# Latent up projection: rotary columns of q's weights stored twice, rotation in two operations, k's plain columns scaled on POOL, rotary squares inside k's sum

## The chip, the cores and the metric

The kernel runs on one core of a Trainium2 chip. The core has five engines that work side by side, each with its own queue of instructions that it takes in order: TensorE (PE, matrix products; its weight loads are shown as PEld), VectorE (DVE), ScalarE (ACT), GpSimd (POOL) and SyncE (SP), which here issues the transfers between the chip's main memory and the on-chip memory SBUF. Matrix products land in a second on-chip memory, PSUM, which POOL does not read in this kernel.

The metric is the time of one execution in microseconds (us), median of several runs. Before the change it is 1326.62 us (3 runs, 1322.44 to 1329.13).

## The reference

One layer of a streaming encoder, batch 1, sequence 1024, width 1024: an adaptive normalisation, a mixer with two groups of heads (latent attention "mla" and banded chunk attention), and a gated MLP with a causal convolution. The change lies in how q and k of the latent attention are made:

```python
MLA_HEADS = 8; MLA_NOPE = 64; MLA_ROPE = 32; MLA_QK = 96

q = jnp.dot(rmsnorm(q_lat, g_q_latent), w_q_up).reshape(B, S, MLA_HEADS, MLA_QK)
kv = jnp.dot(rmsnorm(kv_lat, g_kv_latent), w_kv_up).reshape(B, S, MLA_HEADS, MLA_NOPE + MLA_V)
k_nope, v = kv[..., :MLA_NOPE], kv[..., MLA_NOPE:]
k = jnp.concatenate([k_nope, jnp.broadcast_to(k_rope[:, :, None, :], (B, S, MLA_HEADS, MLA_ROPE))], axis=-1)
q = rmsnorm(q, g_mla_q)
k = rmsnorm(k, g_mla_k)
q = jnp.concatenate([q[..., :MLA_NOPE], rope(q[..., MLA_NOPE:], positions)], axis=-1)
k = jnp.concatenate([k[..., :MLA_NOPE], rope(k[..., MLA_NOPE:], positions)], axis=-1)

def rope(x, positions):          # half = 16 columns
    x1, x2 = x[..., :half], x[..., half:]
    return jnp.concatenate([x1 * cos - x2 * sin, x2 * cos + x1 * sin], axis=-1)
```

`rmsnorm(y, g)` is `y * rsqrt(mean(y*y) + eps) * g`. A head of q has 64 plain columns and 32 rotary ones. The rotary part of k is one row of 32 columns that all heads share. Since the norm multiplies a whole head's row by one number, the rotation may be done before or after that multiplication.

## The kernel before

The kernel works in stages. First come the adaptive shift and scale and the first projections. Then follows a long stage of attention (some 80 to 610 us of the profiled span), in which units of attention and "fillers" are mixed: a unit is four blocks of 128 queries of one head, and the fillers are the remaining projections, cut into steps. `pace` draws filler steps in proportion to the matrix work of the attention just issued; `need` draws all of a filler that a unit depends on. The order in which each engine gets its instructions is then planned from estimated costs, with a priority for attention (`tc.high_priority`). Last come the output projection and the MLP.

The fillers are, in order, projections for the chunk heads, then `f_m` (the latents: q's and kv's low-rank rows, and k's rotary row `kr`, rotated, with the sum of its squares in `ssr`), then `f_up(0)` and `f_up(1)`, which the change touches, then `f_oca` (part of the output projection). `f_up(gr)` makes q, k and v of four latent heads, `gr` being the first or second four; the first unit of the first four heads needs `f_up(0)`, the later ones `f_up(1)`.

Products of 32-bit numbers are made of three passes: every factor is split in a high part (ACT, `hi_of`, L77) and a low part (POOL or DVE, `lo_of`, L84), and `gemm3_f` issues high x high, high x low and low x high (L154, L155, L156).

`f_up(gr)` first loads and splits its weights: `w_qu` (two tiles of 128x384, from L637) and `w_kvu` (128x512, L643). Then it goes through eight tiles of 128 rows. For each:

- `qu`: the q product, 2 x 3 matmuls of 384 columns into a PSUM tile. ACT copies it to `uqr` (L664) and squares it into `usq` (L666); DVE sums the squares of each head (L669).
- `ku`: the k and v product, 3 matmuls of 512 columns. ACT copies the plain columns of k to `kraw` (L675) and squares them (L677); DVE sums them (L678) and adds k's rotary sum `ssr` (L679).
- The root: POOL takes the eight sums to the power -0.5 (`rsqrt_mean`, L119 and L120), giving `ur`.
- v: ACT writes its 16-bit high part (L682), DVE its low part (L683).
- q: DVE multiplies all 384 columns by the root (L685), and then rotates 32 columns of each of four heads in four DVE operations (`rope_apply`: two products, L497 and L498, a difference, L499, and a sum, L500).
- k: DVE multiplies the plain columns (L689) and the rotary row (L690) by the root.

The buffers of `uqr` and `kraw` are of one kind ("R", four of them), so two tiles are in flight. The squares use a ring of two buffers, which the weights' loads use as well. The results, `qn` and `kn`, are transposed on PE when an attention unit begins (`mq_ps` and `mk_ps`, L729), split again (`mq_0h`, `mq_1l`, `mk`, L737, L738, L741, L742), and used in the scores `sm`. In attention itself POOL scales the probabilities (L73, `hlm`) and DVE makes their low part (L851). The factors of the rotation, `tabq` for q and `tabk` for k, are made once by `rope_tables` (L611): 32 columns of cosines and 32 of sines, each with the norm's gain.

Of the kernel before, what the change touches and what calls it, by code (L numbers as in the profile page):

```python
# [24 lines left out]
P = 128  # L25
D = 1024
S = 1024
NT = S // P
# [36 lines left out]
def layer_kernel(ctx, tc, I, out):  # L65
# [473 lines left out]
    def rope_tables():  # L539
# [67 lines left out]
        for tab, c0 in ((tabq, C_RQ), (tabk, C_RK)):  # L607
            for half, trig in ((0, cn), (1, sn)):
                for j in range(2):
                    o = half * 32 + j * 16  # L610
                    dve.tensor_tensor(tab[:, :, o:o + 16], trig,  # L611
                                      pk[:, c0 + j * 16:c0 + j * 16 + 16].unsqueeze(1)
                                      .to_broadcast([P, NT, 16]), op=MUL)
                    yield
# [13 lines left out]
    def f_up(gr):  # L628
# [6 lines left out]
        for k in range(2):  # L635
            raw = qtile(f"wqr{gr}_{k}")
            sp.dma_start(raw[:, :384], I["w_qu"][gr][:, k, :])  # L637
            w = g4([P, 2, 512], F32R, f"wq{gr}_{k}")
            hi_of("a", w[:, 0, :384], raw[:, :384])
            lo_of("p", w[:, 1, :384], raw[:, :384], w[:, 0, :384])  # L640
# [12 lines left out]
        for t in range(NT):  # L653
            h, j = divmod(t, 4)
            sl = slice(j * P, (j + 1) * P)
            if t % 2 == 0:
# [4 lines left out]
            yield from gemm3_f(pt[:, :384], [(latT[k, h][:, 0, sl], latT[k, h][:, 1, sl], wq[k][:, 0, :384], wq[k][:, 1, :384])  # L661
                                for k in range(2)])
            rq = rtile(f"uqr{gr}_{t}")
            act.activation(rq[:, :384], pt[:, :384], AF.Copy)  # L664
# [12 lines left out]
            act.activation(s3, r3, AF.Square)  # L677
            dve.tensor_reduce(ss[:, 4:8], s3, axis=AX.X, op=ADD)  # L678
            dve.tensor_tensor(ss[:, 4:8], ss[:, 4:8], ssr[:, t:t + 1].to_broadcast([P, 4]), op=ADD)  # L679
# [5 lines left out]
            dve.tensor_tensor(q_t, rq[:, :384].rearrange("p (a b) -> p a b", a=4),  # L685
                              r[:, 0:4].unsqueeze(2).to_broadcast([P, 4, QK]), op=MUL)
            rope_apply(q_t[:, :, NOPE:], q_t[:, :, NOPE:], tabq, t, 4, rq[:, 0:256], dve)
            k_t = mk[gr, t // 2][:, t % 2]
            dve.tensor_tensor(k_t[:, :, 0:NOPE], r3, r[:, 4:8].unsqueeze(2).to_broadcast([P, 4, NOPE]), op=MUL)  # L689
# [897 lines left out]
def _inputs(a):  # L1587
# [32 lines left out]
    v = ca[:, :, 2].reshape(ND, P, 2, 256).transpose(2, 1, 0, 3)  # L1620
    wa = f("w_ada")
# [32 lines left out]
```

## Time and profile before

| | |
|---|---|
| median of 3 runs | 1326.62 us (1322.44 to 1329.13) |
| the profiled execution | 1326.91 us |
| its span, first to last instruction | 1325.1 us |
| mean granted PE clock | 0.961 of full speed |
| busy, whole span | PE 90%, PEld 75%, DVE 82%, ACT 47%, POOL 44% |
| up projection, first product | 340.7 us |
| last tile's rotation ends | 453.6 us |

Times are in microseconds from the span's start unless marked ns. A row of a group gives the line, engine and operation, the tile written and the tiles read, partitions x elements of output and input, the count, then busy time and the mean of one in ns, then the engine's idle time before it. A row of a tile gives the shortest, middle and longest of its instructions in ns. A row in order of time gives start and length, and in brackets how long the engine stood idle before it and what ended that wait. A row of waits gives who waited for whom, the total, the number of times and the longest.

### The profile page before, as it was taken

The numbers are of one execution on the slowest core, as the hardware profiler recorded it, in microseconds if no ns is written. First come the engines' busy times: TensorE is split into PE (matmuls) and PEld (weight loads), VectorE is DVE, ScalarE is ACT, GpSimd is POOL, SyncE is SP. The second block draws the span as 40 slices with busy tenths as digits, with TensorE's granted clock in tenths as the row PEclk, the third lists the DMA queues.
The fourth block names the chain that finished last, engine by engine and source line by source line (L and its number), as shares of the span: only waits on it lengthen the run. The fifth ranks groups of instructions, "written<-read, shape, count | busy, mean of one in ns | idle before, by whom it ended". The sixth has DMA issues, their size and how long they took to land.

```text
span 1325.1 us, 18721 instructions
## 1 busy us (share of the span) xinstructions
PE 1191.0 (90%) x6168; PEld 992.2 (75%) x6168; DVE 1086.5 (82%) x1928; ACT 623.6 (47%) x1132; POOL 580.7 (44%) x613
## 2 busy tenths in 40 slices
PE   3899899888678788878899999999999998999998
PEld 3789888878556577756677888888888886888886
DVE  6979989887699978774789888888889886687667
ACT  5454654364556444452476444443444444433331
POOL 5485773586567643344515445454444431000000
PEclk9899899999879898888999999999999998999999
DMA  8416769665124677679602333333243336943441
GB/s 323 144 55 149 169 146 198 154 166 121 28 80 80 150 162 140 139 153 324 260 16 80 127 104 133 114 109 126 94 133 104 128 103 243 394 135 116 128 160 63
DMA packets 223689, 190.57 MB, mean 144 GB/s; under 512 B 148708, under 2 KB 166884, under 8 KB 223592
## 3 DMA queue, kind: packets, MB, share of 16 engines
q1 hardware_dynamic: 223592, 189.38, 49.9%
q8 instruction: 48, 0.79, 0.2%
q14 instruction: 49, 0.40, 0.1%
HBM read 117.24 MB, written 37.49 MB: 117 GB/s over the span
## 4 chain that ended last, share of the span: by engine, by line
PE 50%; DVE 4%; DMA 3%; issue 2%; ACT 1%; POOL 1%; SPq 0%; POOLq 0%; DVEq 0%; ACTq 0%
PE p L1130 10%; PE p L1131 10%; PE p L1132 10%; PE dnA_P L1465 2%; PE dnA_P L1467 2%; PE dnA_P L1466 2%; DMA PTm<-hlm 2%; PE dnB_P L1467 2%; PE dnB_P L1465 2%; PE dnB_P L1466 2%; PE dnA L1465 1%; PE dnA L1466 1%; PE dnA L1467 1%; PE sm L803 1%; PE dnB L1467 1%
## 5 line engine op out<-in xcount | busy, mean ns | idle before, releaser
L77 ACT ACTIVATE dnP<-dnr 128x1024 fp32r<-128x1024 f32 x73 | 77.5, 1064 | 117.3 <-PE dnA_P L1467 46.3
L1439 DVE TENSOR_TENSOR dnP<-dnr,dnP 128x1024 fp32r<-128x1024 f32 x72 | 87.9, 1223 | 52.7 <-ACT dnP L77 52.7
L73 POOL TENSOR_SCALAR hlm<-Pm,rim 128x512 f16<-128x512 f32 (+2 forms) x96 | 68.8, 728 | 85.7 <-DVE rim L832 45.6
L84 POOL TENSOR_TENSOR wf<-wu,wf 128x512 fp32r<-128x512 f32 x22 | 38.7, 1758 | 116.2 <-ACT wf L77 116.2
L84 POOL TENSOR_TENSOR wb<-wu,wb 128x512 fp32r<-128x512 f32 x22 | 44.7, 2033 | 84.9 <-ACT wb L77 57.1
L1301 DVE SCALAR_TENSOR_TENSOR u<-c,cvp,u 128x1023 f32<-128x1023 f32 x44 | 55.8, 1309 | 27.8 <-ACT u L1300 23.7
L891 PE MATMUL pvm<-PTm,vt 128*128 128x256 f16 (+1 forms) x320 | 47.9, 302 | 27.1 <-DMA PTm<-hlm 27.0
L851 DVE SCALAR_TENSOR_TENSOR hlm<-Pm,rim,hlm 128x512 f16<-128x512 f32 (+2 forms) x96 | 66.3, 708 | 6.0 <-POOL hlm L73 5.8
L73 POOL TENSOR_SCALAR hlc<-Pc,ric 128x640 f16<-128x640 f32 (+2 forms) x64 | 48.8, 764 | 47.0 <-DVE ric L832 17.8
L829 ACT ACTIVATE Pc<-sc,mc 128x640 f32<-128x640 f32 (+2 forms) x64 | 42.2, 660 | 54.9 <-DVE mc L818 36.9
L891 PEld LDWEIGHTS <-vt 128*128 128x128 f16 x320 | 32.9, 111 | 42.3 <-issue 21.2
L829 ACT ACTIVATE Pm<-sm,mm 128x128 f32<-128x128 f32 (+3 forms) x64 | 47.2, 738 | 35.1 <-DVE sm L821 9.7
L1300 ACT ACTIVATE u<-c,cvp 128x1024 f32<-128x1024 f32 x44 | 52.3, 1238 | 23.6 <-DVE c L1399 16.5
L77 ACT ACTIVATE wc<-ws 128x512 fp32r<-128x512 f32 x21 | 13.3, 632 | 92.9 <-DVE ws L1149 87.1
L851 DVE SCALAR_TENSOR_TENSOR hlc<-Pc,ric,hlc 128x640 f16<-128x640 f32 (+2 forms) x64 | 50.9, 801 | 7.0 <-POOL hlc L73 6.8
L154 PE MATMUL ipq<-wq_s,hT 128*128 128x256 f32 x192 | 56.2, 293 | 0.0
L1302 DVE SCALAR_TENSOR_TENSOR u<-c,cvp,u 128x1022 f32<-128x1022 f32 x44 | 55.5, 1300 | 0.0
L155 PE MATMUL ipq<-wq_s,hT 128*128 128x256 f32 x192 | 55.0, 286 | 0.0
L156 PE MATMUL ipq<-wq_s,hT 128*128 128x256 f32 x192 | 54.9, 286 | 0.0
L1466 PE MATMUL dnA_P<-dnP 128*128 128x512 f32 x132 | 51.3, 389 | 0.0
L1467 PE MATMUL dnA_P<-dnP 128*128 128x512 f32 x132 | 51.3, 389 | 0.0
L1465 PE MATMUL dnA_P<-dnP 128*128 128x512 f32 x132 | 51.2, 389 | 0.0
(443 smaller groups left out, 4399.7 us busy)
## 6 DMA issues: line engine op xcount, KB each, us to landing
wu<-w_up SPq DMA_DIRECT2D x44, 512.0 KB, 3.5
dnr<-g_d SPq DMA_DIRECT2D x73, 256.0 KB, 2.7
aw<-w_ada SPq DMA_DIRECT2D x48, 256.0 KB, 3.3
g_d<-u SPq DMA_DIRECT2D x22, 512.0 KB, 2.8
dnr<-w_down SPq DMA_DIRECT2D x44, 256.0 KB, 5.4
adaw<-w_ada_a SPq DMA_DIRECT2D x16, 512.0 KB, 6.4
x<-x SPq DMA_DIRECT2D x16, 512.0 KB, 9.0
g_d<-gs SPq DMA_DIRECT2D x22, 256.0 KB, 2.7
```

Source lines behind the costliest of these rows:

```text
L73: pool.tensor_scalar(o, i, s, 1.0, op0=MUL, op1=MUL)
L77: act.activation(o, i, AF.Copy)
L84: (pool if eng == "p" else dve).tensor_tensor(o, i, f32(hi), op=SUB)
L829: act.activation(pr[:, :n], sv, AF.Exp, bias=m[:], scale=-1.0, accum_out=rsum[:, 0:1])
L851: dve.scalar_tensor_tensor(hl[:, w:2 * w], pp, ri[:], hl[:, :w], op0=MUL, op1=SUB)
L1130: pe.matmul(pt, sh, pg[:, 0], start=(k == 0 and not add), stop=False, skip_group_check=skip)
L1131: pe.matmul(pt, sh, pg[:, 1], start=False, stop=False, skip_group_check=skip)
L1132: last = pe.matmul(pt, sl, pg[:, 0], start=False, stop=(k == 3), skip_group_check=skip)
L1439: r = f(*a, **k)
L1465: pe.matmul(pt, sh, w[:, 0, 0], start=start, stop=False, skip_group_check=add)
L1466: pe.matmul(pt, sh, w[:, 1, 0], start=False, stop=False, skip_group_check=add)
L1467: pe.matmul(pt, sl, w[:, 0, 0], start=False, stop=stop, skip_group_check=add)
```

## The change

Host side, the q weights get 32 more columns a head: the rotary columns once more, with their halves swapped, so that a head has 128 columns and a tile's product 512:

```diff
+    qu = f("w_q_up").reshape(2, P, 2, 4, QK)
+    qu = np.concatenate([qu, qu[..., NOPE + 16:], qu[..., NOPE:NOPE + 16]], axis=-1)
...
-        "w_qu": f("w_q_up").reshape(2, P, 2, 384).transpose(2, 1, 0, 3),
+        "w_qu": qu.reshape(2, P, 2, 512).transpose(2, 1, 0, 3),
```

The sines in q's table are stored in swapped order and with the first half negated (the table's operation becomes a `scalar_tensor_tensor` of the same shape). One product of the 64 columns with the table, and one sum of its two halves, are then the rotated columns. They are formed in `uqr` itself, before the root. The squares still read 96 columns of each head.

For k, the rotary sum `ssr` is written by ACT into a 65th column beside the squares of each head, so the sum over 65 columns contains it and the separate addition goes; `kraw` grows from 512 to 516 columns. The multiplication of k's plain columns by the root moves from DVE to POOL.

```diff
-            sp.dma_start(raw[:, :384], I["w_qu"][gr][:, k, :])
+            sp.dma_start(raw[:], I["w_qu"][gr][:, k, :])
             w = g4([P, 2, 512], F32R, f"wq{gr}_{k}")
-            hi_of("a", w[:, 0, :384], raw[:, :384])
-            lo_of("p", w[:, 1, :384], raw[:, :384], w[:, 0, :384])
+            hi_of("a", w[:, 0], raw[:])
+            lo_of("p", w[:, 1], raw[:], w[:, 0])
...
-            yield from gemm3_f(pt[:, :384], [(latT[k, h][:, 0, sl], latT[k, h][:, 1, sl], wq[k][:, 0, :384], wq[k][:, 1, :384])
+            yield from gemm3_f(pt[:], [(latT[k, h][:, 0, sl], latT[k, h][:, 1, sl], wq[k][:, 0], wq[k][:, 1])
                                 for k in range(2)])
             rq = rtile(f"uqr{gr}_{t}")
-            act.activation(rq[:, :384], pt[:, :384], AF.Copy)
+            act.activation(rq[:], pt[:], AF.Copy)
+            rq4 = rq[:].rearrange("p (a b) -> p a b", a=4)
             sq = qtile(f"usq{gr}_{t}")
-            act.activation(sq[:, :384], rq[:, :384], AF.Square)
+            act.activation(sq[:, :384].rearrange("p (a b) -> p a b", a=4), rq4[:, :, :QK], AF.Square)
...
+            dve.tensor_tensor(rq4[:, :, NOPE:], rq4[:, :, NOPE:],
+                              tabq[:, t:t + 1, :].to_broadcast([P, 4, 64]), op=MUL)
+            dve.tensor_tensor(rq4[:, :, NOPE:QK], rq4[:, :, NOPE:QK], rq4[:, :, QK:], op=ADD)
...
-            raw = rtile(f"kraw{gr}_{t}")
+            raw = rtile(f"kraw{gr}_{t}", (P, 516))
...
-            s3 = raw[:, 256:512].rearrange("p (a b) -> p a b", a=4)
-            act.activation(s3, r3, AF.Square)
+            s3 = raw[:, 256:516].rearrange("p (a b) -> p a b", a=4)
+            act.activation(s3[:, :, NOPE], ssr[:, t:t + 1].to_broadcast([P, 4]), AF.Copy)
+            act.activation(s3[:, :, :NOPE], r3, AF.Square)
             dve.tensor_reduce(ss[:, 4:8], s3, axis=AX.X, op=ADD)
-            dve.tensor_tensor(ss[:, 4:8], ss[:, 4:8], ssr[:, t:t + 1].to_broadcast([P, 4]), op=ADD)
...
-            dve.tensor_tensor(q_t, rq[:, :384].rearrange("p (a b) -> p a b", a=4),
-                              r[:, 0:4].unsqueeze(2).to_broadcast([P, 4, QK]), op=MUL)
-            rope_apply(q_t[:, :, NOPE:], q_t[:, :, NOPE:], tabq, t, 4, rq[:, 0:256], dve)
+            dve.tensor_tensor(q_t, rq4[:, :, :QK], r[:, 0:4].unsqueeze(2).to_broadcast([P, 4, QK]), op=MUL)
...
-            dve.tensor_tensor(k_t[:, :, 0:NOPE], r3, r[:, 4:8].unsqueeze(2).to_broadcast([P, 4, NOPE]), op=MUL)
+            pool.tensor_tensor(k_t[:, :, 0:NOPE], r3, r[:, 4:8].unsqueeze(2).to_broadcast([P, 4, NOPE]), op=MUL)
```

More of the change, by code (lines that the diff above doesn't have):

```diff
@@ L610, in rope_tables @@
                     o = half * 32 + j * 16
-                    dve.tensor_tensor(tab[:, :, o:o + 16], trig,
-                                      pk[:, c0 + j * 16:c0 + j * 16 + 16].unsqueeze(1)
-                                      .to_broadcast([P, NT, 16]), op=MUL)
+                    swap = half == 1 and tab is tabq
+                    g0 = c0 + (1 - j if swap else j) * 16
+                    dve.scalar_tensor_tensor(tab[:, :, o:o + 16], trig, -1.0 if swap and j == 0 else 1.0,
+                                             pk[:, g0:g0 + 16].unsqueeze(1).to_broadcast([P, NT, 16]),
+                                             op0=MUL, op1=MUL)
                     yield
```

## The prediction

> **What bounds the kernel now.** I read the page's first lines, then the busy times by stage, then the groups of instructions inside the stage that the change touches, and last its order of time. The page:
>
> ```profile
> span 1325.1 us, 18721 instructions
> PE 1191.0 (90%) x6168; PEld 992.2 (75%) x6168; DVE 1086.5 (82%) x1928; ACT 623.6 (47%) x1132; POOL 580.7 (44%) x613
> ```
>
> Over the whole span TensorE is the busiest engine, but that average says nothing of the up projection. Its 16 tiles (two groups of 8) run from 343 to 456 us. Busy time by stage; the columns are the stage, its length, PE, PEld, DVE, ACT, POOL, granted clock, DMA share, GB/s:
>
> ```profile
> 348.84:359.60 10.76, 7.19 (x30) 4.80 (x30) 9.69 (x34) 6.22 (x16) 6.02 (x6) 1.00 0.00 0
> 343.00:361.40 18.40, 13.45 (x58) 9.46 (x57) 15.07 (x50) 12.02 (x30) 9.33 (x10) 0.99 0.00 1
> 361.40:377.40 16.00, 9.12 (x36) 6.32 (x35) 14.48 (x51) 9.59 (x26) 9.52 (x11) 0.79 0.17 46
> 377.40:391.40 14.00, 11.51 (x47) 9.08 (x47) 13.20 (x30) 7.58 (x19) 12.47 (x12) 0.75 0.41 116
> 391.40:456.00 64.60, 48.76 (x242) 36.72 (x241) 61.86 (x185) 35.56 (x82) 41.76 (x43) 0.87 0.48 98
> 456.00:606.00 150.00, 123.87 (x688) 97.85 (x687) 115.48 (x276) 70.85 (x146) 61.32 (x79) 0.90 0.73 153
> ```
>
> In the up stage DVE leads: 90% in the steady part of the first group (9.69 of 10.76), 94% and 96% while the second group shares it with the first attention units of the latent heads, against 75% (48.76 of 64.60) for PE at a clock of 0.87. After 456 no engine is full (PE 83%, DVE 77%); what ends there is a chain that simply starts earlier if the up stage ends earlier. So DVE's time in 343 to 456 is what counts.
>
> The groups that the change touches, in 343 to 456 (name, count, then busy us and mean ns), and the shortest, middle and longest of the same instructions:
>
> ```profile
> L689 DVE TENSOR_TENSOR kn<-kraw,ur 128x256 f32<-128x256 f32 x16 | 8.4, 526 | 0.0
> L500 DVE TENSOR_TENSOR qn<-uqr 128x64 f32<-128x64 f32 x16 | 5.7, 359 | 0.0
> L498 DVE TENSOR_TENSOR uqr<-qn,tabq 128x128 f32<-128x128 f32 x16 | 5.5, 345 | 0.0
> L499 DVE TENSOR_TENSOR qn<-uqr 128x64 f32<-128x64 f32 x16 | 5.0, 314 | 0.1
> L497 DVE TENSOR_TENSOR uqr<-qn,tabq 128x128 f32<-128x128 f32 x16 | 5.0, 314 | 0.0
> L679 DVE TENSOR_TENSOR uss<-uss,ssr 128x4 f32<-128x4 f32 x16 | 3.8, 239 | 0.0
> ...
> L689 DVE TENSOR_TENSOR kn<-kraw,ur x16: 403/417/1492, 348.3 to 447.6; 128x256 f32<-128x256 f32 x16
> L500 DVE TENSOR_TENSOR qn<-uqr x16: 158/227/1297, 349.6 to 453.4; 128x64 f32<-128x64 f32 x16
> L498 DVE TENSOR_TENSOR uqr<-qn,tabq x16: 264/279/1347, 349.1 to 450.2; 128x128 f32<-128x128 f32 x16
> L499 DVE TENSOR_TENSOR qn<-uqr x16: 195/213/1169, 349.4 to 453.3; 128x64 f32<-128x64 f32 x16
> L497 DVE TENSOR_TENSOR uqr<-qn,tabq x16: 265/281/680, 348.9 to 448.4; 128x128 f32<-128x128 f32 x16
> L679 DVE TENSOR_TENSOR uss<-uss,ssr x16: 140/152/1237, 345.6 to 443.9; 128x4 f32<-128x4 f32 x16
> ```
>
> Their means are far above their medians. The order of time shows why, with POOL's splitting of weights beside two multiplications:
>
> ```profile
> 377.53 1.62 DVE L685 TENSOR_TENSOR qn<-uqr,ur 128x384 f32<-128x384 f32 x1
> 379.07 1.49 DVE L689 TENSOR_TENSOR kn<-kraw,ur 128x256 f32<-128x256 f32 x1
> ...
> 377.46 1.28 POOL L84 TENSOR_TENSOR wk<-wkr,wk 128x512 fp32r<-128x512 f32 x1
> 378.69 1.59 POOL L84 TENSOR_TENSOR wo<-wor,wo 128x512 fp32r<-128x512 f32 x1
> ```
>
> L685 starts 0.07 us after POOL's subtraction and ends only after it (379.15 against 378.74): a DVE operation with both inputs in SBUF stands still while POOL streams a large operand. Median to mean, the six removed operations lose 2097 - 1569 = 528 ns a tile in this way.
>
> **The change part by part.** *DVE, removed and added.* Per tile go L689, L497 to L500 and L679; by medians 417+281+279+213+227+152 = 1569 ns, by means 2097 ns. Added are one 128x256 multiplication (as L689, 417 ns) and one 128x128 addition (as L497, 281 ns): 698 ns. Net 871 ns by medians. Consecutive DVE records overlap by some 0.09 us (L689 below starts at 359.06, L685 ends at 358.60 + 0.55), and four instructions fewer lose four such overlaps, so the net can be as low as 0.55 us; I take 0.70 us a tile, 11.2 us over 16 tiles, bounds 8.8 and 13.9. The removed waits for POOL (528 ns x 16 = 8.4 us) I count at nothing: most would fall on the next two-input operation; the upper bound takes half of them.
>
> *First group: a ring, not only DVE.* Two tiles are in flight, since four buffers serve `uqr` and `kraw`. One turn for one tile:
>
> ```profile
> 352.40 0.49 ACT L664 ACTIVATE uqr<-qu 128x384 f32<-128x384 f32 x1 [1.43 <-DVE kn L689]
> 354.69 0.41 DVE L678 TENSOR_REDUCE uss<-kraw 128x4 f32<-128x256 f32 x1
> 356.01 0.15 DVE L679 TENSOR_TENSOR uss<-uss,ssr 128x4 f32<-128x4 f32 x1
> 356.71 1.64 POOL L120 TENSOR_TENSOR ur<-uss,nhalf 128x8 f32<-128x8 f32 x1
> 356.75 0.24 DVE L500 TENSOR_TENSOR qn<-uqr 128x64 f32<-128x64 f32 x1
> 358.60 0.55 DVE L685 TENSOR_TENSOR qn<-uqr,ur 128x384 f32<-128x384 f32 x1
> 359.06 0.42 DVE L689 TENSOR_TENSOR kn<-kraw,ur 128x256 f32<-128x256 f32 x1
> 359.58 0.49 ACT L664 ACTIVATE uqr<-qu 128x384 f32<-128x384 f32 x1 [1.43 <-DVE kn L689]
> ```
>
> 359.58 - 352.40 = 7.18 us for two tiles, 3.59 each. In the new ring L679 is gone, which waited behind the previous tile's multiplications: the root can begin at about 355.1 and not 356.16, 1.06 us earlier. A buffer comes free at the end of L685, 0.33 us before that of L689. ACT adds 0.13 us (wider copy) and 0.2 us (the copy of the rotary sums), prices below. That gives 7.18 - 1.06 - 0.33 + 0.33 = 6.1 us; the two rotation operations may stand before the reduction (up to 0.7) and POOL's new multiplication may hold L685 up (up to 0.6): 6.1 to 7.4, a middle of 6.6, 3.3 us a tile, 0.28 less than now. DVE alone would allow 3.59 - 0.70 = 2.89, so the ring takes over as the bound. Five such tiles up to 361.4 give 1.4 us (0 to 2.5).
>
> *POOL, added.* The nearest row is the same multiplication with twice the columns; beside it the other prices:
>
> ```profile
> L356 POOL TENSOR_TENSOR qn<-raw,r x12: 1041/1046/1627, 117.8 to 272.2; 128x512 f32<-128x512 f32 x12
> L155 PE MATMUL qu<-wq,latT x32: 335/337/522, 341.2 to 425.8; 128*128 128x384 f32 x32
> L155 PE MATMUL ku<-wk,latT x16: 391/397/776, 343.2 to 430.3; 128*128 128x512 f32 x16
> 454.20 0.58 ACT L718 ACTIVATE co<-oc 128x512 f32<-128x512 f32 x1
> 330.05 0.21 ACT L519 ACTIVATE msq<-lat 128x32 f32<-128x32 f32 x1
> ```
>
> For 256 columns between half, 0.52, and the whole, 1.05; part of an instruction is fixed, so 0.6 us, 9.6 us in all. POOL has room (41.76 of 64.60), but it takes turns in order: behind the multiplication stand the scaling of attention's probabilities and the next tile's root. It becomes ready when the root ends, on the same engine, and so just before L685 on DVE, which waits for that root too and has two SBUF inputs. If POOL comes first, L685 loses up to 0.6 us; where DVE is late anyway, nothing. I take half, 0.3 us, in the nine tiles from 377 on, 2.7 us.
>
> *361 to 456.* Three tiles in 361 to 377.4, where DVE is busy 14.48 of 16: 3 x 0.70 x 0.6 = 1.3 us. From 377.4 on nine tiles (the last one of the first group and eight): 9 x 0.70 = 6.3 us less DVE work, less 2.7 for POOL; but here the lock waits fall on fewer operations, of which I credit a third, 9 x 0.528 / 3 = 1.6. Of the 5.2 that remain I take all, since DVE stands at 95%. The rotation also leaves the end of q's path: it now precedes the root. Waiting for it now:
>
> ```profile
> PE mq_ps L729 <- DVE qn L500: 5.7, 3, 2.5
> ```
>
> Three waits of 5.7 us in all, the longest 2.5; each ends some 1.0 us sooner (the four rotation operations, 1000 ns by medians), but DVE is the bound here too, so I add 1.0 us, bounds 0 and 4.
>
> *PE, ACT, DMA.* Six matmuls a tile have 512 columns and not 384: by the L155 rows 60 ns each, 0.36 us a tile, 5.8 us of PE, beside a PE that is idle a quarter of the stage. It shows only where a group starts: 0.4 us twice, and 0.3 for the wider split of the first weights. I take 0.8 us lost, bounds 0 and 2. ACT's copy grows from 0.49 to about 0.6 and the extra copy costs 0.21 us: 0.33 us a tile where ACT is busy 55% (35.56 of 64.60); beyond the ring it costs nothing, and without DVE as cover 16 x 0.33 = 5 us at most. The transfers of `w_qu` grow by a third and remain ahead of their use; the eight operations of the rotary tables keep their shapes, zero.
>
> Sum: 1.4 + 1.3 + 5.2 + 1.0 - 0.8 = 8.1 us. The profiled execution took 1326.91 us, its span and 1.8 around it, 0.3 above the median of 1326.62; 1326.9 - 8.1 = 1318.8, against the median 1318.5.
>
> The Trainium skill's "SBUF — State Buffer", section "Who interferes with whom", says that the port pair which GpSimd shares with VectorE is an exclusive lock: a VectorE operation with two SBUF inputs and a GpSimd operation that reads SBUF block one another for the whole instruction. The rows at 377 agree. The row at 356.75 does not: L500, with two SBUF inputs, took 0.24 us inside a root of 1.64 us. By the rule applied in full, each of the 16 multiplications on POOL would take an estimated 0.6 us from DVE.
>
> **The rivals.** *Partly eaten gain.* Every new POOL multiplication holds DVE for its whole 0.6 us, so a tile gains 0.70 - 0.60 = 0.1 us, 1.6 us in all; with 1.0 from q's path and 0.8 lost at the starts, about 1.8 us remain: 1324.8. The Trainium skill's rule named above leads here. Ring and lock together at their middle, with no gain in the second group's attention, give 1.4 + 1.3 + 1.5 - 0.8 = 3.4: 1323.2. For it: both operations wait for the same root. Against: DVE at 95% seldom waits at L685 itself.
>
> *Slower: POOL's turn becomes the bound.* The multiplication is queued on POOL ahead of attention's scaling and the next root. If it also waits for DVE (as the subtraction at 378.69, 1.59 us against 1.28 for the one before), a tile loses 0.6 on DVE and 0.6 before the next root, against 0.70 gained: 0.5 x 16 = 8 us, 1334.6. It decides once the stalls pass 0.70 + 6.6/16 = 1.1 us a tile. Against: the largest single stall now is 1.62 - 0.55 = 1.07 us, and POOL has a third of the stage free.
>
> *Another order.* The order of instructions is planned with estimated costs; fewer DVE operations and longer matmuls shift the interleaving with attention up to 606. A loss of a tenth of the 78.6 us from 377 to 456 would take back the gain: 1326.6. Nothing in the trace shows which way it falls.
>
> *Larger gain.* If the lock waits go too (half of 8.4) and all of 0.87 us a tile counts, 13.9 + 4.2 - 2.7 = 15.4 us: 1311.2.
>
> **How the numbers follow.** A measurement of this kernel can tell about 0.5%, 6.6 us, from no change: faster means below 1320.0, slower above 1333.2. Forecast (0.44, 1314 to 1322, of which four fifths lie below 1320.0, 0.36), larger gain (0.14), partly eaten (0.20), another order (0.09, of which 0.03 slower), POOL's turn (0.13). Faster 0.36 + 0.14 = 0.50; slower 0.13 + 0.03 = 0.16; the rest, 0.34, within. The range runs from 1310, under the larger gain, to 1331, which leaves out the slower cases alone.
>
> **What would show it.** Between 343 and 456: L497 to L500 and L679 gone from DVE, two rotation operations of about 0.42 and 0.28 us; the first group's tiles 3.2 to 3.4 us apart; DVE's busy time in the stage 10 to 20 us lower; the stage's end some 8 us earlier with the later stages unchanged in length. Wrong would be: L685 above 1 us on average beside POOL's multiplication (the lock), long POOL waits in front of the root, or a longer stage from 456 to 606 (the order).

## The result and the profile after

The changed kernel takes 1320.31 us (median of 9 runs, 1317.34 to 1323.50), the kernel before 1326.62 us (9 runs in the same comparison). The ratio is 0.996, with a 95% interval of 0.9944 to 0.9976: between 3.2 and 7.4 us of 1326.6 are gained. Two profiled executions of this same changed kernel, whose instructions stand in the same order, begin the same work up to 2.8 us apart (the first split of q's weights at 333.57 and at 335.43, the first copy of a q product at 343.97 and at 346.77), so a difference of less than 3 us between the starting times of two traces carries nothing below. Lengths repeat better: four tiles of the first group take 13.19 and 13.12 us in the two.

The page of the kernel after, its first lines:

```profile
span 1318.7 us, 18701 instructions
...
PE 1192.2 (90%) x6168; PEld 993.5 (75%) x6168; DVE 1080.2 (82%) x1864; ACT 627.3 (48%) x1148; POOL 597.4 (45%) x629
```

DVE has 64 instructions fewer (four a tile) and 6.3 us less to do, POOL 16.7 us more. Now busy times by stretch, before and after, with the same columns as in the prediction (stretch, length, PE, PEld, DVE, ACT, POOL, clock, DMA share, GB/s); the last row of each runs from the first product of q to the end of attention in its own trace, so that both hold the same work. Before:

```profile
343.00:377.00 34.00, 22.17 (x92) 15.38 (x91) 29.27 (x99) 21.20 (x53) 18.45 (x20) 0.90 0.08 22
377.00:456.00 79.00, 60.67 (x288) 46.19 (x289) 75.35 (x215) 43.55 (x102) 54.62 (x55) 0.85 0.46 100
340.71:606.69 265.98, 209.69 (x1075) 162.10 (x1075) 221.72 (x597) 136.43 (x302) 135.19 (x154) 0.88 0.56 120
```

After:

```profile
343.00:377.00 34.00, 25.71 (x92) 17.42 (x90) 27.44 (x78) 21.77 (x60) 23.80 (x28) 0.85 0.07 24
377.00:456.00 79.00, 67.12 (x306) 51.46 (x306) 69.85 (x172) 45.41 (x110) 61.73 (x63) 0.83 0.46 100
341.68:598.64 256.96, 208.31 (x1077) 160.41 (x1075) 212.01 (x533) 139.79 (x318) 147.63 (x170) 0.90 0.59 125
```

From 343 to 456 DVE falls from 104.62 to 97.29 us, 7.3 us; over the same work, by the last rows, from 221.72 to 212.01, 9.7 us. It is still the fullest engine from 377 on (88%), but PE (85%) and POOL (78%) have moved up beside it.

The new instructions, shortest, middle and longest in ns:

```profile
L673 DVE TENSOR_TENSOR uqr<-uqr,tabq x16: 398/415/772, 346.6 to 432.1; 128x256 f32<-128x256 f32 x16
L675 DVE TENSOR_TENSOR uqr<-uqr x16: 268/276/1267, 347.6 to 435.7; 128x128 f32<-128x128 f32 x16
L691 DVE TENSOR_TENSOR qn<-uqr,ur x16: 526/638/1625, 350.1 to 437.8; 128x384 f32<-128x384 f32 x16
L693 POOL TENSOR_TENSOR kn<-kraw,ur x16: 610/836/1469, 349.8 to 440.6; 128x256 f32<-128x256 f32 x16
```

Now the end of attention and the output projection. PE's last product of attention and the first and last product of the output projection, before:

```profile
603.60 3.09 PE L891 MATMUL pvm<-PTm,vt 128*128 128x256 f16 x16 [3.91 <-DMA PTm<-hlm]
607.18 0.50 PE L154 MATMUL op<-wo,oh 128*128 128x512 f32 x1 [0.50 <-ACT oh L77]
657.29 0.39 PE L156 MATMUL op<-wo,ol 128*128 128x512 f32 x1
```

After:

```profile
595.33 3.31 PE L895 MATMUL pvm<-PTm,vt 128*128 128x256 f16 x16 [4.55 <-DMA PTm<-hlm]
598.75 0.50 PE L154 MATMUL op<-wo,oh 128*128 128x512 f32 x1
652.41 0.39 PE L156 MATMUL op<-wo,ol 128*128 128x512 f32 x1
```

Attention ends at 606.69 before and at 598.64 after, 8.05 us earlier. The last product of the output projection is only 4.9 us earlier: from its first to its last product that stage grew from 50.1 to 53.7 us. What follows keeps about that distance, and the spans differ by 6.4 us. So by these traces the up projection and attention gave what was forecast, and the output projection took 3.2 us of it back. What happened there stands in SyncE's order of time. Before:

```profile
609.62 0.46 SPq L903 DMA_DIRECT2D oT_d<-om  x1
610.12 1.08 SPq L1169 DMA_DIRECT2D x<-x  x2
```

After, with the row of its waits that belongs to it:

```profile
602.52 0.46 SPq L907 DMA_DIRECT2D oT_d<-om  x1
610.11 0.81 SPq L1173 DMA_DIRECT2D x<-x  x2
...
SPq L1173 <- DMA oT_d<-om: 7.0, 1, 7.0
```

The first row of each is the store of the last attention output, the second the load of the layer's input `x` that is added to the projection's result. Before, the load is issued 0.5 us behind the store. After, it waits 7.0 us until the store has landed, and starts at 610.11 as if nothing had been gained. In the built program the reason is an address. The last output tile takes one of the four "R" buffers. After, it is the fourth, at bytes 40864 to 42912 of each partition, and the first tile of `x` begins at 42496. Before, it was the third, at 38720 to 40768. That the buffers grew from 2048 to 2064 bytes (the 516 columns of `kraw`) isn't the reason: with the old size the fourth would have reached from 40768 to 42816 and overlapped as well, and the kernel with the joined squares alone, whose buffers have grown too, puts its last tile into the third, at 38784 to 40832, and issues the load 0.5 us behind the store (604.18 and 603.68). Which of the four the last tile gets differs from kernel to kernel.

Not all of what the output projection lost is that wait. The loads of attention's output that stand behind `x` in SyncE's queue begin 10.5 us after the stage's first product before, and 14.7 us after; from its first to its last product PE waits 3.8 us for split factors before, and 6.7 after, 2.9 of the 3.6 us by which the stage grew. The rest goes with the granted clock, 0.97 in this stage before and 0.94 after. Two kernels whose load does not wait, but whose clock there is 0.91, took 52.0 and 52.1 us from first to last product (the kernel before with the tile moved, and the rotation alone; both below).

### The profile page after: what moved, and what is told of

It is laid out like the page before. It is cut to its first block, busy times and chain, and to the rows that moved or that the text cites. A ratio compares the mean times of both kernels' runs of the same rounds, so it can differ in the third digit from the quotient of the medians.

```text
span 1318.7 us, 18701 instructions
## 1 busy us (share of the span) xinstructions
PE 1192.2 (90%) x6168; PEld 993.5 (75%) x6168; DVE 1080.2 (82%) x1864; ACT 627.3 (48%) x1148; POOL 597.4 (45%) x629
## 5 line engine op out<-in xcount | busy, mean ns | idle before, releaser
L73 POOL TENSOR_SCALAR hlm<-Pm,rim 128x512 f16<-128x512 f32 (+3 forms) x96 | 67.9, 716 | 66.7 <-issue 22.5
L855 DVE SCALAR_TENSOR_TENSOR hlm<-Pm,rim,hlm 128x512 f16<-128x512 f32 (+3 forms) x96 | 68.7, 728 | 6.4 <-POOL hlm L73 6.2
L895 PE MATMUL pvm<-PTm,vt 128*128 128x256 f16 (+1 forms) x320 | 43.6, 284 | 22.6 <-DMA PTm<-hlm 21.6
L1304 ACT ACTIVATE u<-c,cvp 128x1024 f32<-128x1024 f32 x44 | 52.4, 1238 | 23.6 <-DVE c L1403 16.7
L77 ACT ACTIVATE wc<-ws 128x512 fp32r<-128x512 f32 x21 | 13.3, 632 | 93.1 <-DVE ws L1153 87.2
```

Source lines behind the costliest of these rows:

```text
L73: pool.tensor_scalar(o, i, s, 1.0, op0=MUL, op1=MUL)
L77: act.activation(o, i, AF.Copy)
L855: dve.scalar_tensor_tensor(hl[:, w:2 * w], pp, ri[:], hl[:, :w], op0=MUL, op1=SUB)
L895: last = pe.matmul(dst, u.vst(j), mov, start=(x == 0), stop=(x == len(todo) - 1), skip_group_check=True)
```

## The experiments

Theory 1 is the prediction's: DVE's time in the up projection counts, and POOL's new multiplication gives back half of its own time by holding DVE. Its rival is the full lock: DVE stands still for all of that multiplication. (The lock is that of the prediction: a DVE operation with two inputs in SBUF and POOL's operation do not run side by side.) Theory 3 came out of the two traces: the load of `x` that waits for a store took back 3 us or so. All runs were timed against the kernel before on their own chip (its median there: 1326.67 for the first four, 1325.76 for the next four, 1324.93 for the last four), so ratios are compared.

### Each part alone

**The rotation alone.** The changed kernel with the other two parts undone.

```diff
-            pool.tensor_tensor(k_t[:, :, 0:NOPE], r3, r[:, 4:8].unsqueeze(2).to_broadcast([P, 4, NOPE]), op=MUL)
+            dve.tensor_tensor(k_t[:, :, 0:NOPE], r3, r[:, 4:8].unsqueeze(2).to_broadcast([P, 4, NOPE]), op=MUL)
...
+            dve.tensor_tensor(ss[:, 4:8], ss[:, 4:8], ssr[:, t:t + 1].to_broadcast([P, 4]), op=ADD)
```

> The rotation part alone: q's rotary columns twice, two rotation operations before the root; k's plain columns stay on DVE and k's rotary sum is added by DVE as before. Theory 1 (DVE is the bound of the up stage): by the rows of before L497 to L500 go (1000 ns) and 698 ns come, 0.30 to 0.40 us of DVE a tile, 16 tiles, 5 to 6 us, and 1 us less wait for q's last operation, less 0.8 us for longer matmuls at the starts: 1321 to 1323. Rival (the ring of four buffers and attention's own chain are the bound, DVE's gain is not passed on): within 2 us of before, 1325 to 1328. In both, the last store of attention does not share memory with the first load of x, so that load is not held.

Measured: 1322.49 us, ratio 0.9964 (0.9949 to 0.9979): 4.8 us gained, as theory 1 has it.

**POOL's multiplication alone.** The kernel before with L689 on POOL.

```diff
-            dve.tensor_tensor(k_t[:, :, 0:NOPE], r3, r[:, 4:8].unsqueeze(2).to_broadcast([P, 4, NOPE]), op=MUL)
+            pool.tensor_tensor(k_t[:, :, 0:NOPE], r3, r[:, 4:8].unsqueeze(2).to_broadcast([P, 4, NOPE]), op=MUL)
```

> Only the multiplication of k's plain columns moved to POOL; the rest as before. Theory 1 (POOL's multiplication takes half of its time back from DVE): 0.34 to 0.42 us of DVE saved a tile, 0.3 us lost, near nothing over 16 tiles: 1325 to 1327. Rival (the lock in full: DVE loses the whole of the multiplication, 0.6 to 0.86 us a tile): 16 x 0.2 to 0.45 us lost, 1330 to 1334. A third (POOL's time is free): 1320 to 1321.

Measured: 1324.79 us, ratio 0.9986 (0.9973 to 0.9999): 1.9 us gained, at most 3.6. A loss of several us is excluded, and so is a free move.

**The joined squares alone.** The kernel before with the 65th column.

```diff
-            s3 = raw[:, 256:512].rearrange("p (a b) -> p a b", a=4)
-            act.activation(s3, r3, AF.Square)
+            s3 = raw[:, 256:516].rearrange("p (a b) -> p a b", a=4)
+            act.activation(s3[:, :, NOPE], ssr[:, t:t + 1].to_broadcast([P, 4]), AF.Copy)
+            act.activation(s3[:, :, :NOPE], r3, AF.Square)
...
-            dve.tensor_tensor(ss[:, 4:8], ss[:, 4:8], ssr[:, t:t + 1].to_broadcast([P, 4]), op=ADD)
```

> Only k's rotary sum as a 65th column of the squares, the addition on DVE gone. Theory 1: DVE saves 0.15 us a tile and the root starts 1 us earlier in the first group, where a tile then takes about 3.2 to 3.4 us in place of 3.59: 1.5 to 4 us, 1322.5 to 1325. Rival (only DVE's work counts): 16 x 0.08 to 0.15 us, 1 to 2.5 us, and the first group's tiles stay within 0.1 us of 3.59 less 0.15.

Measured: 1326.73 us, ratio 1.0009 (0.9989 to 1.0028): nothing gained that could be measured, 1.5 us at most. Theory 1's 1.5 to 4 us are missed, although the ring did get shorter in this kernel's trace, as the last section of the experiments shows.

### The load that waits for a store

The changed kernel with the last attention output in another ring of SBUF buffers (`pgtile`, ring "pg", six buffers). The order of instructions is the same on every engine.

```diff
-                    dst = rtile(f"o{u.nm}_{u.g}") if final else \
+                    dst = pgtile([P, 512], F32, f"o{u.nm}_{u.g}") if final else \
```

> The changed kernel with one buffer elsewhere: the tile of attention's last output, which in the changed kernel lies across the memory of the first tile of x, so that the load of x waits for that output's store to land (7.0 us on SyncE's queue in its trace), is taken from another ring. The order of instructions on every engine is the same. Theory 3 (this wait gives back part of the gain between the end of attention and the first MLP product): the load starts about 7 us earlier, the first MLP product about 3 us earlier, 1316 to 1318. Rival (the output projection is held by the landing of other loads, the wait is hidden): the same as the changed kernel, 1319.5 to 1321.

Measured: 1313.39 us (5 runs), ratio 0.9904 (0.9889 to 0.9919). Theory 3 holds in its direction, with a larger size than expected. SyncE and PE in this kernel, called the mended kernel from here on:

```profile
597.56 0.46 SPq L907 DMA_DIRECT2D oT_d<-om  x1
598.06 1.08 SPq L1173 DMA_DIRECT2D x<-x  x2
...
595.18 0.50 PE L154 MATMUL op<-wo,oh 128*128 128x512 f32 x1
645.12 0.39 PE L156 MATMUL op<-wo,ol 128*128 128x512 f32 x1
```

The load is issued 0.5 us behind the store again, and the output projection takes 49.9 us from first to last product, against 50.1 before the change.

Two controls followed. The first is the changed kernel once more, unchanged, beside other runs:

> The changed kernel itself, as a control on the same chip as the three others. If the load of x that waits for the last attention store is worth what the trace of the changed kernel shows (3.2 us given back in the output projection), this stands 3 to 4 us above e4_slot, and e4_slot's further lead of 3.5 us over the first measurement was spread between runs: 1316 to 1317.5. If that lead belongs to the slot, 1319 to 1321.

Measured: 1320.07 us, ratio 0.9958 (0.9941 to 0.9975), the first measurement again. Its output projection:

```profile
599.29 0.80 PE L154 MATMUL op<-wo,oh 128*128 128x512 f32 x1
651.91 0.39 PE L156 MATMUL op<-wo,ol 128*128 128x512 f32 x1
```

It takes 52.6 us from first to last product. The second control is the same edit in the kernel before:

```diff
-                    dst = rtile(f"o{u.nm}_{u.g}") if final else \
+                    dst = pgtile([P, 512], F32, f"o{u.nm}_{u.g}") if final else \
```

> The kernel before with the last attention tiles in the other ring, order unchanged: the edit that made e4_slot out of the changed kernel. In the kernel before the load of x did not wait for the last store, so theory 3 (the edit is worth what that wait costs) expects no change: 1325 to 1328. Rival (the other ring is better by itself, by the 3 us or so of e4_slot's lead that arose before the attention's end): 1322 to 1324.

Measured: 1325.52 us, ratio 1.0001 (0.9988 to 1.0014). The other ring is worth nothing by itself; it pays only where the address held the load. By the ratios (0.9958 and 0.9904) the edit is worth 0.54% or 7.2 us, give or take 3; the traces show 2.7 to 3.7 us of it in the output projection. The remaining 3 us or so arise, in the one trace of the mended kernel, before attention's end, where the edit changes no instruction and no order. What differs there is the granted clock: 0.93 from the first product of q to attention's end, against 0.90 and 0.91 in the two traces of the changed kernel. Over whole executions the five of the mended kernel show 0.964 to 0.971, the twelve of the control 0.955 to 0.971. Executions of both at the same clock (0.964, 0.969 and 0.971) are 4.7, 2.5 and 2.5 us apart, and 0.9 more if the medians of the kernel before on their two chips are set equal. So the wait itself is worth an estimated 3 to 6 us; why the clock was higher isn't shown.

### Leaving one part out of the mended kernel

With that wait gone, the three parts together gain 12.7 us (0.9904), more than twice the 4.8 + 1.9 - 1.2 us of the single ones. So each was taken out of the mended kernel.

**Without POOL's part**: the multiplication `kn` back on DVE.

```diff
-            pool.tensor_tensor(k_t[:, :, 0:NOPE], r3, r[:, 4:8].unsqueeze(2).to_broadcast([P, 4, NOPE]), op=MUL)
+            dve.tensor_tensor(k_t[:, :, 0:NOPE], r3, r[:, 4:8].unsqueeze(2).to_broadcast([P, 4, NOPE]), op=MUL)
```

> The kernel is e4_slot with the multiplication of k's plain columns (kn) back on DVE. In the changed kernel that multiplication was 0.84 us of POOL and took about 0.3 us a tile from DVE by my theory (port shared), against the 0.6 us or so that it costs on DVE itself. Theory 1 (POOL's work gives back half of what it takes): moving it back costs about 0.1 to 0.3 us in each of some 9 tiles that DVE bounds, so 1 to 3 us slower than e4_slot: 1314 to 1316.5. Rival (full lock: DVE stands still for all of POOL's multiplication): moving it back is free or a gain of 2 us: 1311 to 1313. Rival (POOL's work is free): 16 x 0.6, of which 9 x 0.6 = 5.4 us is lost: 1318 to 1319.

Measured: 1314.15 us, ratio 0.9923 (0.9899 to 0.9948): 2.5 us slower than the mended kernel by the ratios, but the intervals overlap. With them POOL's part is worth 2.5 us, give or take 3.9, which doesn't tell it from nothing.

**Without the joined squares**: L679 back, ACT's copy gone.

```diff
-            act.activation(s3[:, :, NOPE], ssr[:, t:t + 1].to_broadcast([P, 4]), AF.Copy)
...
+            dve.tensor_tensor(ss[:, 4:8], ss[:, 4:8], ssr[:, t:t + 1].to_broadcast([P, 4]), op=ADD)
```

> The kernel is e4_slot without the part that joins the rotary squares to k's sum: the 128x4 addition on DVE (L679 in the kernel before, 0.15 us by the median, 0.24 by the mean) stands behind the reduction again, and ACT's 0.20 us copy is gone. Theory 1 (the addition lies on the ring of the first group and takes DVE time in the second): 16 x 0.15 to 0.24 us of DVE and the ring's wait, 2 to 5 us slower than e4_slot, 1315.5 to 1318.5. Rival (this part is worth nothing, as it was alone): 1312.5 to 1314.5.

Measured: 1315.94 us, ratio 0.9924 (0.9906 to 0.9942): 2.6 us slower, within theory 1's range, but give or take 3.1, again with overlapping intervals.

**Without the rotation**: the kernel before with POOL's multiplication, the joined squares and the mended ring.

```diff
-            dve.tensor_tensor(k_t[:, :, 0:NOPE], r3, r[:, 4:8].unsqueeze(2).to_broadcast([P, 4, NOPE]), op=MUL)
+            pool.tensor_tensor(k_t[:, :, 0:NOPE], r3, r[:, 4:8].unsqueeze(2).to_broadcast([P, 4, NOPE]), op=MUL)
...
+            act.activation(s3[:, :, NOPE], ssr[:, t:t + 1].to_broadcast([P, 4]), AF.Copy)
```

> The kernel before with kn on POOL and the joined squares, and the last attention tiles in the other ring as in e4_slot, but with the four rotation operations in their old place: e4_slot without the rotation part. Theory 1 (the rotation carries most of the gain: 0.30 us a tile of DVE, and it leaves the path between the root and the transposes, 1.0 us): 6 to 9 us slower than e4_slot, 1319.5 to 1322.5. Rival (the gain lies in the ring of the first group, which the join and POOL shorten): 1315 to 1318.

Measured: 1329.13 us, ratio 1.0024 (1.0011 to 1.0038): slower than the kernel before, and 15.9 us slower than the mended kernel, more than either theory gave. By these times the rotation carries all of the gain in company, though only 4.8 us of it alone. But the granted clock differs too: the twelve executions of this kernel show 0.950 to 0.959, the five of the mended kernel 0.964 to 0.971. Among the 23 to 29 executions of the kernel before on each chip, one with a clock 0.01 higher took 5.2 to 6.7 us less by a straight line through them, so by an estimate 7 to 9 of the 15.9 us go with the difference of the medians, 0.014. Whether the clock is a cause of the longer time here or follows from it, no run shows.

### What POOL's multiplication costs, and whom

**Twice on POOL.** The mended kernel with `kn` issued twice a tile.

```diff
+            pool.tensor_tensor(k_t[:, :, 0:NOPE], r3, r[:, 4:8].unsqueeze(2).to_broadcast([P, 4, NOPE]), op=MUL)
```

> The kernel is e4_slot with POOL's multiplication kn issued twice a tile, with the same result: the suspected cost doubled. Theory 1 (each takes about 0.3 us from DVE in 9 to 16 tiles): 3 to 5 us slower than e4_slot, 1316 to 1318.5. Rival (full lock: 0.8 us a tile): 7 to 13 us slower, 1320 to 1326. Rival (POOL's work costs DVE nothing, and POOL has time): no change, 1313 to 1314.

Measured: 1325.97 us, ratio 1.001 (0.999 to 1.0029): 14.1 us slower than the mended kernel by the ratios. Groups in 335 to 452 us, and a row of the waits:

```profile
L694 POOL TENSOR_TENSOR kn<-kraw,ur 128x256 f32<-128x256 f32 x16 | 13.3, 832 | 0.9
...
L693 POOL TENSOR_TENSOR kn<-kraw,ur 128x256 f32<-128x256 f32 x16 | 11.7, 730 | 0.9
...
ACT uqr L666 <- POOL kn L694: 5.3, 3, 3.3
```

The second multiplication is 13.3 us of POOL; the two together are 25.0, where the mended kernel's one is 13.7, so 11.3 us were added. The 14.1 us, give or take 3.2, hold all of it. That is the size of the full lock on DVE, but DVE isn't where it was spent, as the busy times show below.

**Twice on DVE.** The mended kernel with `qn` issued twice a tile.

```diff
+            dve.tensor_tensor(q_t, rq4[:, :, :QK], r[:, 0:4].unsqueeze(2).to_broadcast([P, 4, QK]), op=MUL)
```

> The kernel is e4_slot with the 128x384 multiplication qn issued twice a tile on DVE, with the same result: 0.55 us more of DVE a tile by its shortest rows, 8.8 us in 16 tiles. Theory 1 (DVE's time bounds the up stage): 5 to 9 us slower than e4_slot, 1318.5 to 1322.5. Rival (POOL's turn with the roots bounds the stage, and the 12.6 us of f7_kn_twice were POOL's own 0.8 us a tile): 0 to 3 us, up to 1316.5.

Measured: 1323.01 us, ratio 0.9991 (0.9974 to 1.0007): 11.5 us slower than the mended kernel by the ratios.

```profile
L691 DVE TENSOR_TENSOR qn<-uqr,ur 128x384 f32<-128x384 f32 x16 | 10.4, 649 | 1.5 <-POOL ur L120 1.5
L692 DVE TENSOR_TENSOR qn<-uqr,ur 128x384 f32<-128x384 f32 x16 | 9.8, 611 | 0.0
...
ACT uqr L666 <- POOL kn L694: 14.2, 8, 4.2
```

The second multiplication is 9.8 us of DVE; the two together are 20.2, where the mended kernel's one, longer beside POOL, is 12.7, so 7.5 us were added. The 11.5 us, give or take 2.9, hold all of it. The rival, by which only POOL's turn counts, is excluded; so is a DVE that alone counts, by the run before.

**On ACT.** The mended kernel with `kn` as four activations, each with one column of the root as its scale, so that neither DVE nor POOL has it.

```diff
-            pool.tensor_tensor(k_t[:, :, 0:NOPE], r3, r[:, 4:8].unsqueeze(2).to_broadcast([P, 4, NOPE]), op=MUL)
+            for j in range(4):
+                act.activation(k_t[:, j, 0:NOPE], r3[:, j], AF.Copy, scale=r[:, 4 + j:5 + j])
```

> The kernel is e4_slot with kn on ACT, as four activations with a scale from the column of r, so that neither DVE nor POOL has it. Theory 1 (DVE bounds the stage after 377 us, and POOL's kn takes 0.3 us a tile from it): 9 x 0.3 = 2.7 us faster than e4_slot, 1309.5 to 1312. Rival (four activations, about 1.1 us of ACT a tile, lengthen the ring of the first group and delay the attention's exponentials): 3 to 5 us slower, about 1317.

Measured: 1308.97 us, ratio 0.9887 (0.9867 to 0.9908). This is the lowest median of the study, 15 us ahead of the kernel before (theory 1's range, 1309.5 to 1312, lies a little above). Against the mended kernel it is 2.3 us, give or take 3.4, with overlapping intervals; against `kn` on DVE, timed in the same round, 4.8 us, give or take 4.2. It takes ACT 17.0 us in all, against the 13.8 us (16 x 859 ns) that the changed kernel's POOL spent on it:

```profile
L694 ACT ACTIVATE kn<-kraw,ur 128x64 f32<-128x64 f32 x64 | 17.0, 339 | 4.6 <-POOL ur L120 4.6
```

ACT had the room: it was busy 55% of 377 to 456 us before (43.55 of 79.00).

Busy times of these kernels from the first product of q to attention's end, columns as above. The changed kernel's second trace and the mended kernel (both `kn` on POOL):

```profile
343.82:599.33 255.51, 207.07 (x1076) 158.92 (x1076) 211.15 (x533) 140.00 (x318) 145.77 (x171) 0.91 0.59 125
341.19:595.12 253.93, 202.01 (x1077) 154.65 (x1075) 212.17 (x533) 139.91 (x318) 148.01 (x170) 0.93 0.60 126
```

With `kn` on DVE:

```profile
341.35:593.15 251.80, 205.99 (x1075) 157.89 (x1075) 205.41 (x545) 136.50 (x313) 138.15 (x154) 0.91 0.58 122
```

With `kn` on ACT:

```profile
342.31:593.48 251.17, 205.11 (x1075) 157.49 (x1075) 204.42 (x533) 153.97 (x382) 135.55 (x154) 0.90 0.60 127
```

With `kn` twice on POOL:

```profile
341.36:605.84 264.48, 211.01 (x1076) 159.15 (x1076) 211.74 (x533) 139.70 (x318) 155.92 (x187) 0.89 0.57 121
```

DVE is busy 211 to 212 us in the three traces with `kn` on POOL and the same order of instructions, and 204.42 with `kn` on ACT, where neither has it on DVE: 7.8 us below the mended kernel, or 0.48 us for each of 16 multiplications. Against the kernel that has `kn` on DVE the mended kernel's DVE is 6.8 us busier, though the other's does the multiplications as well; in 335 to 452 us they are

```profile
L693 DVE TENSOR_TENSOR kn<-kraw,ur 128x256 f32<-128x256 f32 x16 | 8.5, 533 | 0.0
```

which makes (6.8 + 8.5) / 16 = 0.96 us each. With two multiplications on POOL DVE is no busier, 211.74. Three comparisons, three answers: the orders of the instructions differ between these kernels. A lock that adds the whole multiplication to DVE each time is excluded by the last row, since it would have added 11 us or more.

What the lock is stands in the order of time. The changed kernel, two tiles of the first group:

```profile
352.67 0.90 POOL L693 TENSOR_TENSOR kn<-kraw,ur 128x256 f32<-128x256 f32 x1
353.02 0.97 DVE L691 TENSOR_TENSOR qn<-uqr,ur 128x384 f32<-128x384 f32 x1
...
359.55 0.61 POOL L693 TENSOR_TENSOR kn<-kraw,ur 128x256 f32<-128x256 f32 x1
359.67 0.90 DVE L691 TENSOR_TENSOR qn<-uqr,ur 128x384 f32<-128x384 f32 x1
```

`qn` takes 0.55 us by its middle where POOL has no `kn` (the kernel with `kn` on ACT). Here it starts inside POOL's multiplication and ends 0.42 and 0.41 us behind it, and the same two tiles show 0.41 and 0.42 in the second trace and in the mended kernel. So it stood still until POOL was done. POOL can lose as well: its multiplication at 363.53 took 1.39 us and ended 0.46 us behind a `qn` that took its usual 0.55, although by the records POOL's had started first. So in these places one of the two waits the other out, and DVE loses what is left of POOL's multiplication when `qn` starts, not the whole of it.

### The ring of the first group

ACT's copies of the second and the sixth tile, four tiles apart, before:

```profile
345.03 0.49 ACT L664 ACTIVATE uqr<-qu 128x384 f32<-128x384 f32 x1
...
359.58 0.49 ACT L664 ACTIVATE uqr<-qu 128x384 f32<-128x384 f32 x1 [1.43 <-DVE kn L689]
379.30 0.48 ACT L664 ACTIVATE uqr<-qu 128x384 f32<-128x384 f32 x1
```

After, with the ninth tile's copy, the first of the second group, as the last row here and above:

```profile
347.00 0.60 ACT L666 ACTIVATE uqr<-qu 128x512 f32<-128x512 f32 x1 [0.28 <-PE qu L156]
...
360.19 0.60 ACT L666 ACTIVATE uqr<-qu 128x512 f32<-128x512 f32 x1 [0.72 <-POOL kn L693]
381.77 0.60 ACT L666 ACTIVATE uqr<-qu 128x512 f32<-128x512 f32 x1 [1.93 <-PE qu L156]
```

With the joined squares alone:

```profile
342.81 0.49 ACT L664 ACTIVATE uqr<-qu 128x384 f32<-128x384 f32 x1
...
355.81 0.49 ACT L664 ACTIVATE uqr<-qu 128x384 f32<-128x384 f32 x1 [0.27 <-DVE kn L689]
```

And the mended kernel without the joined squares:

```profile
346.42 0.60 ACT L666 ACTIVATE uqr<-qu 128x512 f32<-128x512 f32 x1
...
360.65 0.60 ACT L666 ACTIVATE uqr<-qu 128x512 f32<-128x512 f32 x1 [1.43 <-POOL kn L693]
```

Four tiles take 14.55 us before, 13.19 after, 13.00 with the joined squares alone and 14.23 in the mended kernel without them. So in these two pairs the joined squares shorten the ring, by 1.0 to 1.5 us, as they take an addition out from between the sum and the root. Other kernels don't follow that alone: POOL's multiplication without them takes 13.80, and with them but without the rotation 15.07. Where the gain of the joined squares alone went can't be read from their trace, since the profiled execution (1321.04 us) was the fastest of twelve and itself 5.9 us shorter than that of the kernel before.

## Why the prediction was right, and where it was not

The forecast was 1318.5 us; the kernel takes 1320.31, 1.8 us more. Two of its steps were wrong, in opposite directions, and the sum hides that: that it came so close is in part luck.

- *DVE, removed and added.* The prices were right: 415 and 276 ns by the medians against 417 and 281 forecast. The sign that was named for it, DVE's busy time in the stage 10 to 20 us lower, was missed: it fell by 7.3 us, or 9.7 over the same work. (The lower bound was also added up wrongly: 0.87 less four overlaps of 0.09 is 0.51 us a tile and not 0.55; the value taken doesn't rest on it.) Two operations that stayed became dearer. In 343 to 456 us, before:

```profile
L685 DVE TENSOR_TENSOR qn<-uqr,ur 128x384 f32<-128x384 f32 x16 | 10.6, 663 | 0.5 <-POOL ur L120 0.4
L851 DVE SCALAR_TENSOR_TENSOR hlm<-Pm,rim,hlm 128x512 f16<-128x512 f32 x12 | 9.2, 764 | 0.1
```

  and after:

```profile
L691 DVE TENSOR_TENSOR qn<-uqr,ur 128x384 f32<-128x384 f32 x16 | 12.6, 786 | 0.2 <-POOL ur L120 0.2
L855 DVE SCALAR_TENSOR_TENSOR hlm<-Pm,rim,hlm 128x512 f16<-128x512 f32 x12 | 11.3, 938 | 0.0
```

  `qn` went from 663 to 786 ns on average, `hlm` from 764 to 938, 4.1 us in these two groups. So the third of the old lock waits (1.6 us) that the forecast credited didn't go; more of them came.
- *First group: a ring.* Right in mechanism, and in size with the first copies left out: 14.55 - 13.19 = 1.4 us over four tiles, 3.30 us a tile, where 3.3 and 1.4 us for five were forecast. What was forecast to bring it, L679, brings it in two pairs of kernels, though not in every one. The 0.33 us credited for a buffer that comes free at the end of `qn` did not come as told: the copy at 360.19 waits for POOL's `kn` of 359.55.
- *POOL, added.* Priced at 0.6 us; it took 0.61 at the shortest and 0.84 in the middle, 0.86 on average. That is inside the bounds, above the value taken. Its DVE share was put at 0.3 us; the experiments put it between nothing and 1.0, with 0.48 in the comparison that changes DVE least. The part is worth what the step made of it, little: 1.9 us alone, 2.5 in company, neither much beyond its interval. The Trainium skill's rule of an exclusive lock ("SBUF — State Buffer", "Who interferes with whom") is what the rows at 352.67 and 359.55 show, 0.42 and 0.41 us from POOL's end to the end of `qn`. The rival that leaned on it went wrong elsewhere: it let each multiplication hold DVE for its whole length, while DVE lost only what was left of it.
- *361 to 456.* Split wrongly. Between the sixth tile's copy and the ninth's, where 1.3 us were to be gained, 1.9 were lost (19.72 us before, 21.58 after; 21.67 in the second trace of the same kernel). From the ninth copy to the start of the last `qn`, where some 6 were forecast, more came: 67.7 us before by the last L685 start at 447.0 (379.30 to 447.0), 56.0 after (381.77 to 437.8), 11.7 us. Attention that shares the stage wasn't as much earlier; at its end it was 8.05 us ahead.
- *After 456 "a chain that simply starts earlier".* This step failed, though not as a stretch of DVE or PE that became slower: the load of `x` was not ready to start earlier. It took back up to 3.2 us in the trace, and 7.2 by the mended kernel's ratio, of which an estimated 3 to 6 remain at equal clock. Without it, the forecast's sum would have been too small: the mended kernel gained 12.7 us by its ratio, near the rival of the larger gain (15.4), by other means than that rival named.
- *DVE is the bound.* Half right. A second `qn` cost 11.5 us for 7.5 us more of DVE, as a bound should. But a second `kn` cost 14.1 us for 11.3 more of POOL, which by the prediction's account had a third of the stage free. Either engine's time counts, most likely since both stand in one loop: with four buffers two tiles are in flight, and copy, sum, root and multiplications of a tile follow one another. In that light the move of `kn` to ACT, if its 2.3 us are real, helps for two reasons that these runs don't separate: it leaves POOL's queue, where the next root stands behind it, and it ends the hold on DVE.
- *Another order.* The orders did change, and the prediction had no way to see what that does. The interaction remains open, and the order is one candidate: the rotation is worth 4.8 us alone and 15.9 us beside the other two parts, and those two without it make the kernel 0.24% slower than before, while each alone did no harm that could be measured. The granted clock is another, untested: by the estimate above it goes with about half of the 15.9 us. And in the single traces the stretch from the first product of q to attention's end, 266.0 us before, is 3.7, 5.5 and 3.5 us shorter with one part each and 9.0 and 10.5 with all three, not far from their sum; there only the kernel without the rotation, 1.3 us longer than before, stands out. No run here settles why; it would take the same planned order with other operations in it, which wasn't tried. Nor were more than four "R" buffers.

## What to carry to other kernels

Where tiles go round a ring of few buffers, price what a change does to the whole turn, on every engine it passes, and not to the busiest engine alone: an engine at 78% charged its added time in full here (11.3 us more of POOL, 14.1 us lost), and the engine off the turn's critical part was no worse a place for the work, though it needed more time for it. When orders or buffers change, look at which memory the next stage's first loads share with the tiles that are released last: an overlap of addresses made a load wait for a store and took back some 3 to 7 us of a gain of 13. Parts of a change need not add up: take each out of the whole as well as trying it alone. And compare the granted clock of the runs before explaining a few us between two kernels.

## What the runs showed of the hardware that was not expected

- POOL's 128x256 multiplication took 0.61 us at the shortest and 0.84 us in the middle, more than half of the 1.05 us of the 128x512 one. It and a DVE multiplication with two inputs in SBUF waited each other out: in nine places of the first group, three in each of three traces, a `qn` that started inside it ended 0.41 to 0.42 us behind it; in another POOL's ended 0.46 us behind `qn`.
- A POOL operation does not always hold DVE so: in the trace before, a two-input addition of 128x64 took 0.24 us inside POOL's power of 1.64 us, near its middle of 0.23.
- ACT's multiplication of 128x64 by a column took 0.34 us, four of them 1.36 us against POOL's 0.86 on average for the same 256 columns, and the kernel was no slower for it.
- The store of the last output tile held the next load for 7.0 us, and for 7.4 us in the second trace of the same kernel, where the load had to wait for it.
- Executions of one kernel differ in granted clock, and their time with it: 0.952 to 0.964 and 1328.5 to 1322.9 us among the executions of the kernel before on one chip, 5.2 us for 0.01 by a straight line through its 29.
